# Dense feed-forwards that transpose x unnormalised and take up products of 512 columns

## Chip, cores and metric

The kernel runs on one core of one Trainium2 chip. Times are microseconds of device time for one execution. A time given for a kernel is the median of its runs; a profile is one further execution, whose own time stands beside its span.

## What is computed

256 tokens of 1024 features go through two blocks of two layers each. In the first block a layer is a mixer (a chunked recurrence, gates and a short convolution) and a feed-forward; the feed-forward of layer 0 is dense, that of layer 1 a mixture of 8 experts (MoE). Behind it stands a norm of its own. In the second block a layer is a dense feed-forward, a mixer of four branches and another dense feed-forward, each with a norm before and one after it. So there are five dense feed-forwards, and each is:

```
def rmsnorm(x, g):
    xf = x.astype(jnp.float32)
    y = xf * lax.rsqrt(jnp.mean(xf * xf, axis=-1, keepdims=True) + EPS)
    return (y * g.astype(jnp.float32)).astype(x.dtype)

def swiglu_ffn(h, w_gu, w_down):
    a, b = jnp.split(h @ w_gu, 2, axis=-1)
    return (jax.nn.silu(a) * b) @ w_down
```

with h = rmsnorm(x, g), 1024 features in, 2816 in the middle, 1024 out. All is float32.

## The kernel before

**Products.** Every float32 product is made of three: both operands are split into a high part that TensorE takes without loss and the remainder, and `mm3` (L205 to L209) issues high x high (L207), high x low (L208) and low x high (L209) into one PSUM tile. Weights arrive by SP's queue in raw tiles of 512 KB (`pump`, L111; seven buffers, issue in L124); ACT casts the high part (L139), DVE subtracts for the low part (L141), in pieces of 1024 columns, or two halves of 512 where a feed-forward or mixer begins; six such pairs exist. Activations are split by `split` (ACT L222, DVE L223).

**Layout.** 256 tokens are two tiles of 128 (token tile 0 and 1). A product contracts over 128 rows, so x has to stand with features on the partitions: `hT` is the pair (`hhi`, `hlo`) of eight blocks k of 128 features by 256 tokens.

**Entering a feed-forward.** `norm_next` and `prenorm` compute the mean square (ACT squares, L242; DVE L244), the factor (POOL, L226) and x times factor times gain (DVE L264), with a gain broadcast over the partitions that `gain` (L252 to L254) loads by POOL's queue. `put_hT` transposes four blocks at a time on TensorE (`turn`, L219) into one PSUM tile, which one cast and one subtraction of 512 columns bring into hT. For token tile 1 this is kept as `pend` and run once token tile 0's first products are issued.

**The feed-forward** (`ffn`, L419). The first 256 of 2816 features are computed token by token: hT is stationary, 256 weight columns move, a PSUM tile holds the tokens of one tile. The ten groups of 256 that follow are computed feature by feature: 128 x 128 weights are stationary, the 256 tokens of hT move; so g = silu(a) b comes out with features on the partitions, as the down products want it, and is split into arenas. Only the first group's g has to be transposed (`first_g`, L441). The down products have g as stationary and 512 weight columns moving; the last two chunks of them are done for token tile 0 first, so that its residual add (`add_post` L360, `norm_post` L370 and L373) and the next stage's entry run beside the products of tile 1.

**Out of the MoE.** `final_norm` (L1068) applies two norms in a row behind the add (L1008): squares (L1081), the gain (L1082), small sums on POOL (L1083 and on), squares again (L1091), the normalised x for the feed-forward (L1099), and the new x (L1105).

**Start.** `start` loads x and the first mixer's gain, 512 KB broadcast, then the weights; `enter_first` norms and transposes. `consts` loads small vectors by POOL's queue and turns them into columns.

The order of instructions on every engine is fixed before the run, by a planner that follows the order of the code, with side work (`spawn`, `step`) put later by a set amount of time.

## Time and profile before

| what | us |
|---|---|
| median of 3 runs | 2866.78 (2866.57 to 2866.88) |
| the profiled execution | 2866.45 |
| its span | 2864.7 |
| TensorE busy | 2800.7 (98%) |
| DVE busy | 2025.9 (71%) |
| ACT busy | 1644.8 (57%) |
| POOL busy | 85.7 (3%) |

From the span's start the stages lie at about: first mixer 0 to 322, dense feed-forward to 514, second mixer to 831, MoE to 1654, dense feed-forward to 1861, mixer to 2071, dense feed-forwards to 2263 and 2455, mixer to 2665, dense feed-forward to the end. Of TensorE's matmuls the profile gives starts that can be trusted and ends that are modelled, so the price of a product in a stream is the distance of two starts.

### The profile page before, as it was taken

How to read it: one execution, taken by the hardware profiler on the slowest of the kernel's cores; microseconds unless marked ns; L12 is line 12 of the kernel's file. 1: busy time of each engine (PE TensorE's matmuls, PEld its weight loads, DVE VectorE, ACT ScalarE, POOL GpSimd, SP SyncE). 2: the span in 40 equal slices, each digit the busy share in tenths (PEclk: the TensorE clock that was granted, in tenths of full speed). 3: DMA queues.
4: the chain of work that ended last, by engine and by line, in shares of the span. 5: the costliest groups of instructions: out<-in, count | busy, mean ns of one | idle time of the engine just before them, and what ended most of it. 6: DMA issues, size and time to landing. Idle time of an engine off the chain costs nothing. (4 is left out here: it accounts for less than half of the span.)

```text
span 2864.7 us, 47484 instructions
## 1 busy us (share of the span) xinstructions
PE 2800.7 (98%) x18688; PEld 2553.8 (89%) x18688; DVE 2025.9 (71%) x2639; ACT 1644.8 (57%) x2196; POOL 85.7 (3%) x162
## 2 busy tenths in 40 slices
PE   8999999999999999999999989999999999999999
PEld 8999998999988877877877789899999899899997
DVE  5766655675678888888888765578765555697654
ACT  6644544664458767777777654456544444565543
POOL 1000000000000000000000010100000001000000
PEclk9999999999999999999999989999999999999999
DMA  7554666555558999999999956664665566546553
GB/s 248 161 167 146 185 184 189 179 162 169 171 191 293 327 341 353 333 344 355 330 346 349 338 185 185 187 182 136 193 201 185 191 184 197 170 139 199 182 183 108
DMA packets 425047, 635.00 MB, mean 222 GB/s; under 512 B 20186, under 2 KB 298896, under 8 KB 424816
## 3 DMA queue, kind: packets, MB, share of 16 engines
q1 hardware_dynamic: 421184, 621.65, 67.0%
q0 software_dynamic: 3632, 10.24, 1.3%
q8 instruction: 148, 2.42, 0.4%
q14 instruction: 83, 0.68, 0.1%
HBM read 630.76 MB, written 1.05 MB: 221 GB/s over the span
## 5 line engine op out<-in xcount | busy, mean ns | idle before, releaser
L141 DVE TENSOR_TENSOR wl<-wr,wh 128x1024 fp32r<-128x1024 f32 (+2 forms) x1265 | 1408.3, 1139 | 602.6 <-ACT wh L139 592.5
L139 ACT CAST wh<-wr 128x1024 fp32r<-128x1024 f32 (+2 forms) x1265 | 1200.9, 983 | 626.7 <-PE mm L208 275.1
L207 PE MATMUL mm<-hhi,wh 128*128 128x256 f32 x3360 | 954.5, 284 | 0.0
L208 PE MATMUL mm<-hlo,wh 128*128 128x256 f32 x3360 | 953.2, 284 | 0.0
L209 PE MATMUL mm<-hhi,wl 128*128 128x256 f32 x3360 | 952.6, 284 | 0.0
L207 PEld LDWEIGHTS mm<-hhi,wh 128*128 128x128 f32 x3360 | 643.7, 192 | 1.2 <-issue 1.0
L208 PEld LDWEIGHTS mm<-hlo,wh 128*128 128x128 f32 x3360 | 643.8, 192 | 0.6 <-issue 0.3
L209 PEld LDWEIGHTS mm<-hhi,wl 128*128 128x128 f32 x3360 | 643.8, 192 | 0.6 <-issue 0.3
L208 PE MATMUL mm<-wl,a 128*128 128x512 f32 (+1 forms) x1336 | 514.0, 385 | 2.2
L207 PE MATMUL mm<-wh,a 128*128 128x512 f32 (+1 forms) x1336 | 509.7, 382 | 0.0
L209 PE MATMUL mm<-wh,a 128*128 128x512 f32 (+1 forms) x1336 | 508.5, 381 | 0.0
L208 PEld LDWEIGHTS mm<-wl,a 128*128 128x128 f32 x1336 | 251.3, 188 | 65.9 <-DVE wl L141 17.5
L207 PEld LDWEIGHTS mm<-wh,a 128*128 128x128 f32 x1336 | 251.4, 188 | 49.5 <-issue 1.6
L209 PEld LDWEIGHTS mm<-wh,a 128*128 128x128 f32 x1336 | 251.5, 188 | 45.6
L208 PE MATMUL sd<-wl,a 128*128 128x512 f32 x352 | 144.9, 412 | 1.1
L209 PE MATMUL sd<-wh,a 128*128 128x512 f32 x352 | 140.0, 398 | 5.1 <-PEq L1111 5.1
L207 PE MATMUL sd<-wh,a 128*128 128x512 f32 x352 | 117.4, 399 | 0.0
L222 ACT CAST a<-t 128x256 fp32r<-128x256 f32 (+1 forms) x114 | 49.3, 433 | 108.8 <-DVE t L460 105.4
L207 PE MATMUL mm<-a,wh 128*128 128x256 f32 x384 | 109.3, 285 | 0.0
L208 PE MATMUL mm<-a,wh 128*128 128x256 f32 x384 | 107.6, 280 | 0.0
L209 PE MATMUL mm<-a,wl 128*128 128x256 f32 x384 | 107.6, 280 | 0.0
L209 PE MATMUL mm<-wh,hlo 128*128 128x256 f32 x352 | 103.3, 294 | 3.5 <-DVE hlo L223 3.5
(319 smaller groups left out, 2486.1 us busy)
## 6 DMA issues: line engine op xcount, KB each, us to landing
wr<-in_expert_w_dram SPq DMA_DIRECT2D x515, 512.0 KB, 5.4
wr<-in_w_in_dram SPq DMA_DIRECT2D x240, 512.0 KB, 4.0
wr<-in_ffn_w_gu_dram SPq DMA_DIRECT2D x176, 512.0 KB, 3.7
wr<-in_ffn_w_down_dram SPq DMA_DIRECT2D x88, 512.0 KB, 3.7
wr<-in_dense_w_dram SPq DMA_DIRECT2D x66, 512.0 KB, 3.8
wr<-in_w_out_dram SPq DMA_DIRECT2D x32, 512.0 KB, 4.1
wr<-in_w_proj_conv_dram SPq DMA_DIRECT2D x16, 512.0 KB, 4.3
wr<-in_w_proj_hgrn_dram SPq DMA_DIRECT2D x16, 512.0 KB, 4.2
```

The lines of the kernel that those rows point to most:

```text
L139: nc.scalar.copy(hi[:, c:c + m], raw[:, c:c + m])
L141: nc.vector.tensor_sub(lo[:, c:c + m], raw[:, c:c + m], hi[:, c:c + m].bitcast(F32))
L207: mm(out, l[0], r[0], start=start, stop=False)
L208: mm(out, l[0], r[1], start=False, stop=False)
L209: mm(out, l[1], r[0], start=False, stop=stop)
L222: self.nc.scalar.copy(hi, src)
```

## The change

**Up products.** `UP_COLS` keeps the first 256 features and cuts the rest into five groups of 512. They are computed token by token: hT's 128 tokens are stationary, 512 weight columns move, one PSUM tile for each token tile, first for a, then for b. `stream` takes a piece of weights at a time. g comes out with tokens on the partitions; `turns` transposes it, four blocks into a PSUM tile, and splits it into the arenas, as side work.

**The norm.** `put_scaled` transposes x as it is and multiplies by the gain of a feature when the PSUM tile is read, one 128 x 128 block at a time (ACT `activation` with a scale of its own per partition, L389; DVE L390). The factor of a token is computed beside (`rf`), and enters as scale of the silu (L505) and in the multiplication (L507). `plain_next` does this in place of `norm_next` for the five dense feed-forwards, right behind the add.

**Out of the MoE** `final_norm` does `put_scaled` first, with the product of two gains, then both norms; its small sums move from POOL to DVE. **Start:** the gain comes as eight rows by ACT's queue and is transposed; x is normed without gain and goes through `put_scaled`. **Loads:** `gain` issues on SP's queue; five of its fifteen loads, and the start's, are gone, and `consts` has seven more small loads on POOL's queue instead.

```diff
-        self.nc.gpsimd.dma_start(t, ap.partition_broadcast(P))
+        self.nc.sync.dma_start(t, ap.partition_broadcast(P))
...
-    def enter_first(self, gt):
...
+    def enter_first(self, gain):
+        nc = self.nc
+        def normed(t):
+            r = self.mean_sq([self.x[:, t, h * 512:h * 512 + 512] for h in range(2)])
+            xs = self.t4()
+            for h in range(2):
+                sl = slice(h * 512, h * 512 + 512)
+                last = nc.vector.tensor_scalar_mul(xs[:, sl], self.x[:, t, sl], r)
+            return xs, last.ins
...
+        xs0, self.hold = normed(0)
+        self.pump(1)
+        self.hold = None
+        last = self.hold_act = self.put_scaled(0, gain, xs0)
+        self.pump(4)
+        self.hold_act = None
+        with self.tc.issue_after(last):
+            xs1, _ = normed(1)
+        self.pend = lambda: self.put_scaled(1, gain, xs1)
+        self.pump()
...
+    def put_scaled(self, t, gain, src=None):
+        hi, lo = self.hT
+        for h in range(2):
+            pt = self.sd_ps((P, 4, P))
+            self.turn(pt, (self.x[:, t, :] if src is None else src)[:, h * 512:(h + 1) * 512], 4)
+            for j in range(4):
+                k = 4 * h + j
+                sl = (slice(None), k, slice(t * P, t * P + P))
+                g = gain(k)
+                last = self.nc.scalar.activation(hi[sl], pt[:, j, :], AF.Copy, scale=g)
+                self.nc.vector.scalar_tensor_tensor(lo[sl], pt[:, j, :], g, hi[sl].bitcast(F32), ALU.mult,
+                                                    ALU.subtract)
+        return last.ins
...
+    def plain_next(self, gain):
+        def enter(t):
+            self.put_scaled(t, gain)
+            r = self.mean_sq([self.x[:, t, h * 512:(h + 1) * 512] for h in range(2)])
+            self.nc.vector.tensor_copy(self.rf[t], r)
+        def step(i):
+            if i == 1:
+                self.new_hT()
+                self.new_rf()
+                enter(0)
+            elif i == 2:
+                self.pend = lambda: enter(1)
+        return step
...
+    UP_COLS = [(0, 256)] + [(256 + j * 512, 512) for j in range(5)]
...
-            self.add((n, "a", g), wa[:, :, sl])
-            self.add((n, "b", g), wb[:, :, sl])
+        for g, (c0, cn) in enumerate(self.UP_COLS):
+            self.add((n, "a", g), wa[:, :, c0:c0 + cn])
+            self.add((n, "b", g), wb[:, :, c0:c0 + cn])
         for g in range(KF // 2):
...
+        def swiglu(out, t, a, b):
+            if b is None:
+                nc.scalar.activation(out, a, AF.Silu, scale=rf[t])
+            else:
+                nc.vector.scalar_tensor_tensor(out, b, rf[t], out, ALU.mult, ALU.mult)
...
+        def turns(t, k0, nb, sa):
+            pt = self.sd_ps((P, 4, P))
+            self.turn(pt, sa, nb)
+            yield
+            b = 0
+            while b < nb:
+                i, r = (k0 + b) // 8, (k0 + b) % 8
+                m = min(nb - b, 8 - r)
+                sl = (slice(None), slice(r, r + m), slice(t * P, t * P + P))
+                self.split(G[0][i][sl], G[1][i][sl], pt[:, b:b + m, :])
+                b += m
+            yield
...
-                for p in self.take((n, c, g)):
-                    self.fm_piece([(b, pt[:, j, :]) for b, pt in enumerate(pts)], p, self.hT_all, KD)
...
+        for g, (c0, cn) in list(enumerate(self.UP_COLS))[1:]:
+            sas = [self.t2((P, 512)) for _ in range(NT)]
+            for c in "ab":
+                pts = [self.mm_ps() for _ in range(NT)]
+                for k0, kn, hi, lo in self.stream((n, c, g)):
+                    for t in range(NT):
+                        for kk in range(kn):
+                            k = k0 + kk
+                            self.mm3(pts[t], self.hT_tok(k, t), (hi[:, kk, :], lo[:, kk, :]), k == 0, k == KD - 1)
+                    self.done()
+                for t in range(NT):
+                    if c == "a":
+                        swiglu(sas[t], t, pts[t], None)
+                    else:
+                        swiglu(sas[t], t, None, pts[t])
+                        spawn(t, c0, cn, sas[t])
+                yield
...
-        nc.sync.dma_start(gt, first_gain.partition_broadcast(P))
-        self.pump(2)
+        nc.scalar.dma_start(rows[0:KD, :], first_gain.rearrange("(b p) -> b p", p=P))
+        self.dmas(2)
...
+        gains = (I["norm_ffn"][1], I["norm_ffn"][0], I["ffn1_pre_g_2"][0], I["ffn1_pre_g_2"][1],
+                 I["ffn2_pre_g_2"][0], I["ffn2_pre_g_2"][1])
+        for i, v in enumerate(gains):
+            put(rows1[74 + 8 * i:82 + 8 * i, :], v.rearrange("(b p) -> b p", p=P))
...
+            if nxt is not None:
+                self.put_scaled(t, self.fin_g)
...
-            nc.gpsimd.tensor_scalar(ss[:, 0:1], ss[:, 0:1], ss[:, 1:2], EPS, ALU.add, ALU.add)
+            nc.vector.tensor_scalar(ss[:, 0:1], ss[:, 0:1], ss[:, 1:2], EPS, ALU.add, ALU.add)
...
-            for h in range(2):
-                nc.scalar.activation(junk[:, sl[h]], w[:, sl[h]], AF.Square, scale=1.0 / 32.0, accum_out=sw[:, h:h + 1])
-            nc.gpsimd.tensor_scalar(sw[:, 0:1], sw[:, 0:1], sw[:, 1:2], r, ALU.add, ALU.mult)
-            nc.gpsimd.tensor_scalar(sw[:, 0:1], sw[:, 0:1], r, EPS, ALU.mult, ALU.add)
-            r2 = self.col()
-            self.rsqrt(r2, sw[:, 0:1])
-            nc.gpsimd.tensor_tensor(r2, r2, r, ALU.mult)
-            xs = self.t4()
-            for h in range(2):
...
+                nc.vector.tensor_scalar(sw[:, 0:1], sw[:, 0:1], sw[:, 1:2], r, ALU.add, ALU.mult)
+                nc.vector.tensor_scalar(sw[:, 0:1], sw[:, 0:1], r, EPS, ALU.mult, ALU.add)
+                r2 = self.col()
+                self.rsqrt(r2, sw[:, 0:1])
+                nc.vector.tensor_mul(self.rf[t], r2, r)
```

In a feed-forward's up products TensorE had before, for one group, feature by feature (`mm` the PSUM tile, `wh` and `wl` the weights' parts; the third feed-forward):

```order
L207 MATMUL mm_25088<-hhi_24862,wh_24916 128x256
L208 MATMUL mm_25088<-hlo_24863,wh_24916 128x256
L209 MATMUL mm_25088<-hhi_24862,wl_24917 128x256
L207 MATMUL mm_25088<-hhi_24862,wh_24916 128x256
L208 MATMUL mm_25088<-hlo_24863,wh_24916 128x256
L209 MATMUL mm_25088<-hhi_24862,wl_24917 128x256
L207 MATMUL mm_25088<-hhi_24862,wh_24916 128x256
L208 MATMUL mm_25088<-hlo_24863,wh_24916 128x256
L209 MATMUL mm_25088<-hhi_24862,wl_24917 128x256
```

and has now, in the same feed-forward, token by token (`t` is g of the group before):

```order
L226 MATMUL mm_24495<-wh_24377,hhi_23985 128x512
L227 MATMUL mm_24495<-wl_24378,hhi_23985 128x512
L228 MATMUL mm_24495<-wh_24377,hlo_23986 128x512
L238 MATMUL sd_24403<-ident,t_4557_24249 128x128 x4
L226 MATMUL mm_24496<-wh_24377,hhi_23985 128x512
L238 MATMUL sd_24410<-ident,t_4558_24250 128x128 x4
L227 MATMUL mm_24496<-wl_24378,hhi_23985 128x512
L228 MATMUL mm_24496<-wh_24377,hlo_23986 128x512
L226 MATMUL mm_24496<-wh_24377,hhi_23985 128x512
L227 MATMUL mm_24496<-wl_24378,hhi_23985 128x512
```

Three products of 512 columns take the place of six of 256, and bursts of four transposes stand between them.

At the entry of the same feed-forward (`a` the mixer's arena, `x` the residual stream) TensorE had before:

```order
L209 MATMUL mm_24714<-wh_24746,a_4439_24388 128x512
L207 MATMUL mm_24715<-wh_24746,a_4438_24387 128x512
L208 MATMUL mm_24715<-wl_24747,a_4438_24387 128x512
L209 MATMUL mm_24715<-wh_24746,a_4439_24388 128x512
L219 MATMUL sd_24864<-ident,t_4511_24835 128x128 x4
L219 MATMUL sd_24871<-ident,t_4511_24835 128x128 x4
L207 MATMUL mm_24942<-wh_24764,hhi_24862 128x256
L208 MATMUL mm_24942<-wl_24765,hhi_24862 128x256
L209 MATMUL mm_24942<-wh_24764,hlo_24863 128x256
```

and has now, still among the mixer's last products of token tile 1:

```order
L227 MATMUL mm_23847<-wl_23836,a_4434_23520 128x512
L228 MATMUL mm_23847<-wh_23835,a_4435_23521 128x512
L226 MATMUL mm_23848<-wh_23835,a_4434_23520 128x512
L227 MATMUL mm_23848<-wl_23836,a_4434_23520 128x512
L238 MATMUL sd_23987<-ident,x 128x128 x4
L228 MATMUL mm_23848<-wh_23835,a_4435_23521 128x512
L238 MATMUL sd_24000<-ident,x 128x128 x4
L226 MATMUL mm_23847<-wh_23861,a_4434_23520 128x512
L227 MATMUL mm_23847<-wl_23862,a_4434_23520 128x512
L228 MATMUL mm_23847<-wh_23861,a_4435_23521 128x512
```

The transposes moved from behind the last mixer product to 13 products ahead of it, and read x itself.

DVE had there before:

```order
L373 SCALAR_TENSOR_TENSOR x<-t_4504_24816,col_24822,x 128x512 x2
L141 TENSOR_TENSOR wl_24901<-wr_24665,wh_24900 128x512 x2
L244 TENSOR_SCALAR col_24828<-col_24828 128x1
L141 TENSOR_TENSOR wl_24909<-wr_24685,wh_24908 128x512
L264 SCALAR_TENSOR_TENSOR t_4511_24835<-x,col_24833,gain_22452 128x512 x2
L370 TENSOR_TENSOR t_4516_24878<-mm_24714,gain_22450 128x512
L244 TENSOR_SCALAR col_24879<-col_24879 128x1
L223 TENSOR_TENSOR hlo_24863<-sd_24864,hhi_24862 128x4x128
L370 TENSOR_TENSOR t_4516_24878<-mm_24715,gain_22450 128x512
L223 TENSOR_TENSOR hlo_24863<-sd_24871,hhi_24862 128x4x128
```

and has now:

```order
L448 SCALAR_TENSOR_TENSOR x<-t_4500_23949,col_23955,x 128x512 x2
L150 TENSOR_TENSOR wl_24034<-wr_23798,wh_24033 128x512 x2
L390 SCALAR_TENSOR_TENSOR hlo_23986<-sd_23987,cols,hhi_23985 128x128
L390 SCALAR_TENSOR_TENSOR hlo_23986<-sd_24000,cols,hhi_23985 128x128
L263 TENSOR_SCALAR col_24013<-col_24013 128x1
L150 TENSOR_TENSOR wl_24042<-wr_23818,wh_24041 128x512
L390 SCALAR_TENSOR_TENSOR hlo_23986<-sd_23987,cols,hhi_23985 128x128
L390 SCALAR_TENSOR_TENSOR hlo_23986<-sd_24000,cols,hhi_23985 128x128
L405 COPY rfs<-col_24018 128x1
L150 TENSOR_TENSOR wl_24050<-wr_23839,wh_24049 128x512
L390 SCALAR_TENSOR_TENSOR hlo_23986<-sd_23987,cols,hhi_23985 128x128
L390 SCALAR_TENSOR_TENSOR hlo_23986<-sd_24000,cols,hhi_23985 128x128
```

The subtractions of 512 columns (L223) became eight of 128 (L390), in pairs from two PSUM tiles, with weight splits (L150, before L141) between the pairs; the multiplication by gain and factor (L264) is gone.

Out of the MoE, ACT had before (`x` behind the MoE's add):

```order
L139 CAST wh_20260<-wr_16304 128x512 x2
L139 CAST wh_20274<-wr_16316 128x512 x2
L1081 ACTIVATE t_3861_20340,col_20338<-x 128x512 x2
L139 CAST wh_20288<-wr_16335 128x512
L1091 ACTIVATE t_3861_20340,col_20339<-t_3858_20337 128x512 x2
L139 CAST wh_20288<-wr_16335 128x512
L1105 ACTIVATE x<-t_3858_20337,col_20346 128x1024
L139 CAST wh_20302<-wr_16353 128x512 x2
L139 CAST wh_20316<-wr_16379 128x512
L222 CAST hhi_20358<-sd_20360 128x4x128
L139 CAST wh_20316<-wr_16379 128x512
L222 CAST hhi_20358<-sd_20367 128x4x128
```

and has now:

```order
L148 CAST wh_19846<-wr_15890 128x512 x2
L148 CAST wh_19860<-wr_15902 128x512 x2
L1193 ACTIVATE t_3863_19954,col_19952<-x 128x512
L389 ACTIVATE hhi_19923<-sd_19925,fing 128x128
L148 CAST wh_19874<-wr_15921 128x512
L389 ACTIVATE hhi_19923<-sd_19938,fing 128x128
L148 CAST wh_19874<-wr_15921 128x512
L389 ACTIVATE hhi_19923<-sd_19925,fing 128x128
L389 ACTIVATE hhi_19923<-sd_19938,fing 128x128
L1193 ACTIVATE t_3863_19954,col_19952<-x 128x512
L389 ACTIVATE hhi_19923<-sd_19925,fing 128x128
L389 ACTIVATE hhi_19923<-sd_19938,fing 128x128
```

The evictions of x(0) (L389) moved ahead of the second norm's squares (before L1091, now L1201) and of the new x.

## Rows read from the trace of the kernel before

**Rows 1.** The page's part 1: busy time, share and instructions of TensorE.

```profile
PE 2800.7 (98%) x18688; PEld 2553.8 (89%) x18688; DVE 2025.9 (71%) x2639; ACT 1644.8 (57%) x2196; POOL 85.7 (3%) x162
```

**Rows 2.** Windows, TensorE alone: up products, first dense feed-forward (window, length, busy, clock, DMA).

```profile
322.50:437.60 115.10, 114.39 (x941) 1.00 0.64 187
```

**Rows 3.** One line's instructions, L207, three windows: count, ns min/median/max, first and last start.

```profile
L207 PE MATMUL mm<-hhi,wh x168: 283/283/283, 359.8 to 419.9; 128*128 128x256 f32 x168
...
L207 PE MATMUL mm<-wh,a x21: 389/389/389, 476.0 to 489.6; 128*128 128x512 f32 x21
...
L207 PE MATMUL mm<-wh,a x26: 389/389/389, 495.0 to 512.3; 128*128 128x512 f32 x26
```

**Rows 4.** Timeline of TensorE, first dense feed-forward (start, length, instruction).

```profile
345.59 0.28 PE L209 MATMUL mm<-hhi,wl 128*128 128x256 f32 x1
345.71 0.60 PE L441 MATMUL sd<-ident,t 128*128 128x128 f32 x4
...
346.38 0.29 PE L209 MATMUL mm<-hhi,wl 128*128 128x256 f32 x1
```

**Rows 5.** Timelines of ACT, DVE and TensorE, start (last: idle before, releaser).

```profile
10.21 1.14 ACT L139 CAST wh<-wr 128x512 fp32r<-128x512 f32 x2 [5.36 <-DMA wr<-in_w_in_dram]
...
11.46 1.41 DVE L264 SCALAR_TENSOR_TENSOR t<-x,col,gain 128x512 f32<-128x512 f32 x2
...
12.27 1.97 PE L219 MATMUL sd<-ident,t 128*128 128x128 f32 x8 [12.27 <-DVE t L264]
...
16.25 0.58 PE L209 MATMUL mm<-wh,hlo 128*128 128x256 f32 x1 [0.73 <-DVE hlo L223]
...
19.61 0.41 PE L209 MATMUL mm<-wh,hlo 128*128 128x256 f32 x1
```

**Rows 6.** Out of the MoE: windows, TensorE's waits (us, times, longest), timelines of DVE, TensorE.

```profile
1655.60:1662.10 6.50, 0.02 (x1) 0.71 0.51 160
1662.10:1668.60 6.50, 5.94 (x25) 0.50 0.44 145
...
PE sd L219 <- DVE t L1099: 8.7, 2, 6.5
...
1654.74 1.44 DVE L1008 SCALAR_TENSOR_TENSOR x<-mm,Sc,x 128x512 f32<-128x512 f32 x2 [0.22 <-PE mm L203]
...
1683.57 0.28 PE L209 MATMUL mm<-wh,hlo 128*128 128x256 f32 x1
```

**Rows 7.** Entries behind a mixer: windows, timelines of TensorE and DVE.

```profile
2068.00:2078.00 10.00, 8.82 (x58) 1.00 0.33 104
2261.00:2271.00 10.00, 8.81 (x61) 1.00 0.32 107
2663.00:2673.00 10.00, 8.82 (x60) 1.00 0.31 107
...
2070.23 0.39 PE L209 MATMUL mm<-wh,a 128*128 128x512 f32 x1
2071.55 1.32 PE L219 MATMUL sd<-ident,t 128*128 128x128 f32 x8 [0.94 <-DVE t L264]
...
2073.61 0.38 PE L209 MATMUL mm<-wh,hlo 128*128 128x256 f32 x1 [0.22 <-DVE hlo L223]
...
2066.89 1.42 DVE L373 SCALAR_TENSOR_TENSOR x<-t,col,x 128x512 f32<-128x512 f32 x2
2068.22 1.29 DVE L141 TENSOR_TENSOR wl<-wr,wh 128x512 fp32r<-128x512 f32 x2
```

**Rows 8.** Lines L966, L967 (as rows 3), and a group by form (busy us, mean ns).

```profile
L966 ACT ACTIVATE a<-mm,cols x32: 466/476/493, 840.7 to 1399.9; 128x256 fp32r<-128x256 f32 x32
...
  DVE a L967: 2.4, 3
...
L967 DVE SCALAR_TENSOR_TENSOR a<-mm,cols,a x32: 473/479/484, 841.2 to 1401.6; 128x256 fp32r<-128x256 f32 x32
...
L1600 ACT ACTIVATE t<-t,col 128x128 f32<-128x128 f32 x8 | 3.1, 392 | 0.0
```

More of the change, by code (lines that the diff above doesn't have):

```diff
@@ L107, in add, with dmas, pump @@
         self.plan.append((key, first, len(self.pieces)))
-    def pump(self, limit=1 << 30):
+    def dmas(self, n):
+        for i in range(n):
+            ap, kn, cols = self.raws[i]
+            raw = self.ring.tile([P, RAW], F32, name=self.nm("wr"), tag="wr", bufs=RAW_BUFS)
+            self.nc.sync.dma_start(raw[:, :kn * cols].rearrange("p (k c) -> p k c", c=cols), ap)
+            self.raw[i] = raw
+        self.dma_i = n
+    def pump(self, upto=1 << 30):
         nc = self.nc
+        after = lambda ins: self.tc.issue_after(ins) if ins is not None else nullcontext()
         while True:
             moved = False
-            if self.dma_i >= limit:
-                return
             i = self.dma_i
@@ L138, in pump @@
                     for c in range(0, n, m):
-                        nc.scalar.copy(hi[:, c:c + m], raw[:, c:c + m])
-                        with self.tc.issue_after(self.hold) if self.hold is not None else nullcontext():
+                        with after(self.hold_act):
+                            nc.scalar.copy(hi[:, c:c + m], raw[:, c:c + m])
+                        with after(self.hold):
                             nc.vector.tensor_sub(lo[:, c:c + m], raw[:, c:c + m], hi[:, c:c + m].bitcast(F32))
@@ L170, in take, with stream @@
         return [self.parts.pop(i) for i in range(a, b)]
+    def stream(self, key):
+        k, a, b = self.plan[self.next_i]
+        assert k == key, (k, key)
+        self.next_i += 1
+        for i in range(a, b):
+            self.pump()
+            assert i < self.split_i, (key, i, self.split_i, self.freed)
+            yield self.parts.pop(i)
     def done(self, n=1):
@@ L466, in lhs @@
         def lhs(k, t):
+            for key in [key for key in late if key[0] <= k + 4]:
+                self.finish(late.pop(key))
             hi, lo = g_at(k)
@@ L1656, in build @@
                 self.plan_ffn((kind, l), gu[:, 0:DFF], gu[:, DFF:2 * DFF], I[n + "_w_down_2"][l])
[L1657 to L1661 removed]
+        gain = self.start(I[stages[0][2]][stages[0][1]])
+        self.enter_first(gain)
         late = self.spawn(self.consts())
```

102 lines of the change are left out of this document (47 added, 55 removed).

## Prediction, made before the changed kernel had run

> **What bounds the kernel now.** I read the page's head first: TensorE is busy for 2800.7 of 2864.7 us [rows 1]. So time can only come from two places: from how long the products themselves take, and from the few stretches in which TensorE waits. The five dense feed-forwards are read next. In the first one the up products fill 115.1 us with TensorE busy for 114.39 of them [rows 2]: there is no wait in there to win, only the price of a product. That price is the distance of starts: 168 L207 products with 256 columns start from 359.8 to 419.9, and each is one of three, so 60.1/167/3 = 0.120 us [rows 3]. In the down products of the same feed-forward, 512 columns each, 21 starts lie between 476.0 and 489.6, so 13.6/20/3 = 0.2267 us, and later, on the third pair of arenas, 26 between 495.0 and 512.3, 17.3/25/3 = 0.231 us [rows 3]. Twice 256 columns cost 0.240 us, once 512 cost 0.227 to 0.231. Third, I read the stretches in which TensorE stands: the start, the way out of the MoE, and the entries of the feed-forwards behind a mixer.
>
> **The up products.** Per feed-forward 320 x 3 = 960 products of 256 columns become 480 of 512; the first 256 features stay as they were. Before: 960 x 0.120 = 115.2 us, which is what [rows 2] shows. After, at 0.2267 us: 108.8 us; at 0.231: 110.9 us. Saved: 6.4 or 4.3 us. Which one applies is not shown, as no product of before has 512 columns with the normalised x (hhi, hlo) as its stationary tile. 0.120 and 0.2267 are both the columns at 2.4 GHz (0.107, 0.213) plus 0.013 us, so I take 0.2267.
>
> Against it stand the transposes: g now comes out token by token and is turned back, 44 transposes a feed-forward instead of 4. Four of them in the stream take L209's start at 345.59 to the next L209's at 346.38; three products would have taken 0.36, so four cost 0.79 - 0.36 = 0.43 us, 0.108 each [rows 4]. 40 x 0.108 = 4.3 us. They wait for nothing: in the changed order they stand about 50 products behind the group whose g they turn, some 11 us, in which ACT and DVE have one silu and one multiplication per tile. Net: 6.4 - 4.3 = 2.1 us per feed-forward, 10 us in five; at 0.231 the net is nothing, and at 0.236 (as much again above) five lose 12 us.
>
> The two evictions of a transposed block cost ACT and DVE time, not TensorE's: 1024 columns of weights are split in about the time of two 512-column halves, 1.29 us on DVE [rows 7], and a block of four transposes adds one cast and one subtraction of 512 columns to each engine every 5 us; meanwhile TensorE needs 12 x 0.2267 = 2.7 us for 1024 columns of weights. Neither engine becomes the bound.
>
> The Trainium skill, "TensorE: Matmul & The Clock Gate", section "Back-to-back issue gap", has columns/2.4 GHz + 2.5 ns. By it 960 products would take 104.8 us and 480 would take 103.6: the wider form would save 1.2 us, the transposes would eat it, and five feed-forwards would lose 16 us. By [rows 3] the extra is 0.013 us, so the trace speaks against the rule; it is the fourth rival.
>
> **The start.** TensorE's first real run of products begins at 16.25, behind the norm with a 512 KB gain (L264 at 11.46), the transposes (12.27) and the evictions; it runs at half clock, 16 steps from 16.25 to 19.61, 0.21 us each [rows 5]. The first four blocks (12 products) are done near 18.5. After, no gain is loaded that way; ACT casts the first weights (10.21, 1.14 us [rows 5]) and then does eight evictions. ACT and DVE alternate on a bank: the nearest rows are 0.477 and 0.479 us for 256 columns and 0.392 us for 128 columns on ACT [rows 8], and I take 0.45 for one 128-column eviction with its hand-over. Two banks overlap, so a block of the order k0, k4, k1, k5 comes out every 0.9 us of pairs: k0 is ready at 10.21 + 1.14 + 0.9 = 12.25, k3 at 14.95, its three products end at 15.6. That is 2.9 us sooner than 18.5. The 512 KB that stood ahead of the weights in SP's queue are gone, so the cast itself comes sooner; I add 0.6: 3.5 us. Bounds: nothing, if the small loads of the constants (more of them, on the same POOL queue) stall the products a little later; and 6.0, if the products start at 10.21.
>
> **Out of the MoE.** TensorE does nothing from 1655.6 to 1662.1, then works at half clock to 1668.6, and waits once more behind it; both waits are for L1099, the second norm, 8.7 us in two waits. The last product of the feed-forward's first group starts at 1683.57 [rows 6]. In the new order x(0) is transposed straight after the MoE's add, and both norms run beside the products. x(0) is ready near 1656.2 (L1008, 1654.74 + 1.44). On DVE eight evictions (8 x 0.45) stand with four halves of weight splits (4 x 0.65 [rows 7]) between: 6.2 us behind the first split at 1657.4, so k7 is ready near 1663.5 and tile 0's 48 products end between 1667 (full clock) and 1671 (half). x(1)'s add stands on DVE behind the norm work of tile 0, and its evictions end near 1677; TensorE fills the gap with products of the next group for tile 0, which need nothing of x(1). I put the end of the first group at 1679.8, with 21 products of the next group done (21 x 0.2267 = 4.8 us) where before has three of the old form (0.4). Gain: 3.9 + 4.8 - 0.4 = 8.3 us. Bounds: 4 (the half clock lasts as long as now and x(1) comes as late as now) and 11.
>
> **The entries behind a mixer.** At 2070.23 the last down product starts, at 2071.55 the transposes, at 2073.61 the first lo product [rows 7]. Without waits this last start would be 0.23 + 8 x 0.108 + 0.24 = 1.3 us behind 2070.23; it is 3.4 behind, 2.0 us lost at x(0). The other two entries look the same (8.82, 8.81 and 8.82 us busy in 10 [rows 7]). After, the transposes of x(0) need only the add (L373, 2066.89 to 2068.31) and stand 13 products ahead of the mixer's end, so that wait goes. What is late next: DVE reaches the first eviction at 2069.5, behind a split; with the splits in its order between each two pairs, k2 and k3 come out near 2072.9 and 2074.2, 1.8 us of waits for TensorE. At x(1) I expect what is lost now, less 0.2, as its add is as early as before and its evictions are longer. A gain of 0.4 us each, 1.2 for three; between -2 and +1.5 each. The entry of the first feed-forward, behind the same kind of mixer: nothing, within 1 us. The gains' own loads move from POOL's queue to SP's, where they stand in line with the weights and wait for DVE to free a gain tile; seven raw buffers stand ahead, each the work of 2.7 us, so a wait under some 19 us reaches nobody, and I price it at nothing.
>
> **Sum.** 10.2 + 3.5 + 8.3 + 1.2 = 23.2 us from the profiled execution's 2866.45 gives 2843.3; the median of the runs is 0.3 above it: 2843.5 us.
>
> **Rivals.**
> - The wide products run at 0.231, like the late down products: transposes and products cancel, 10.2 us are missing: 2854. For it: the row exists, in the same feed-forward; against it: only one of three arenas shows it. 0.17.
> - The start and the MoE's way out give nothing, because x(1), the loads or the half clock end last there as they do now: 2843.5 + 11.8 = 2855. For it: half the stretch after 1662.1 is at half clock today whatever is ready. Against it: the waits named are for L264 and L1099, which leave the path. 0.12; together with the first: 2865.5, 0.03.
> - Slower: the small evictions pace every entry. Each of six places (start, MoE, four entries) has two tiles of eight pairs, where two casts and two subtractions stood. At 0.45 us an eviction I have them neutral; if the hand-over between ACT and DVE and the weight splits queued among them make it 0.80, each place loses 8 x 2 x 0.35 = 5.6 us, 33.6 in six: 2877. It decides from 0.45 + 29/96 = 0.75 us on. For it: eight hand-overs a tile stand where there were two; against it: L966 and L967 do just this with 256 columns in 0.48 us, and of 32 casts three waited for L967, 2.4 us together [rows 8]. 0.06.
> - The wide product saves only 0.0025 us on two narrow ones: 0.2375, so 480 take 114.0 us, with the transposes 3.1 more than now, 15.6 in five, instead of 10.2 less: 2869. Against it: no row of 512 columns is above 0.231 [rows 3]. 0.03. It is what the rule of the section "Back-to-back issue gap" of the Trainium skill, "TensorE: Matmul & The Clock Gate", would make of it.
> - A transpose costs more between 512-column products than between 256-column ones: at 0.275 us, 40 x 0.167 = 6.7 us in each feed-forward, 33 us: 2877. Against it: [rows 4]. 0.02. The Trainium skill, "TensorE: Matmul & The Clock Gate", section "Part 4: PE-mode transpose", gives about 275 ns in one kernel's context; this trace has 0.108.
> - The change does more than I see (loads gone from the queue, more products to fill waits): under 2835. 0.05.
>
> **How the numbers follow.** My forecast, 2843.5, between 2835 and 2851 by itself, has 0.52. The range for 8 in 10 reaches down to 2833 and up to 2858, over the first two rivals. A measurement of this kernel can tell 0.2%, 5.7 us, from no change. Faster by more than that (under 2861): 0.52 + 0.17 + 0.12 + 0.05, less 0.02 for the upper ends of the rivals, 0.84. Same: 0.09 (0.03 + 0.03 + 0.02 and a little). Slower: 0.07.
>
> **What would show it.** In the changed profile: the L226 products with 512 columns and hhi as stationary tile 0.227 us apart (0.231: the first rival); a burst of four L238 transposes adding 0.43 us; the up products with their transposes near 113 us per feed-forward instead of 115; TensorE's first products near 12 us and a first wait behind the MoE of about 2 us in place of 6.5; the end of that first group near 1680 less what came before; waits for L389 and L390 of about 2.9 us at an entry. I am wrong if waits for L390 grow past 5 us an entry, or if TensorE's queue waits for SP's weights behind a gain.

## The result, and the profile after

The changed kernel takes 2837.99 us (median of 4 runs, 2836.27 to 2841.31), the kernel before beside it on the same chip 2866.68 (2863.5 to 2866.88): a ratio of 0.9904, with a 95% interval from 0.9887 to 0.9921. That is 28.7 us gained, 5.5 more than the forecast. The time lies inside the range, and what was forecast as likeliest happened. The profiled execution took 2837.38 us with a span of 2835.6, 29.1 less than that of before.

The page's part 1, first line, as [rows 1]: TensorE has 2199 instructions fewer, is still busy for 98%, and gave up 11.2 us of busy time; the other 17.9 us of the shorter span are time in which it stood before.

```profile
PE 2789.5 (98%) x16489; PEld 2445.3 (86%) x16489; DVE 2019.0 (71%) x2635; ACT 1659.0 (59%) x2193; POOL 76.9 (3%) x146
```

**Up products.** Instructions of L226 on TensorE in the first dense feed-forward (as [rows 3]: count, ns, first and last start, shapes), then its timeline there (as [rows 4]: start, length, instruction), in two stretches, without and with a burst of transposes:

```profile
L226 PE MATMUL mm<-wh,hhi x192: 277/389/477, 324.6 to 449.3; 128*128 128x512 f32 x160, 128*128 128x256 f32 x32
```

```profile
355.66 0.39 PE L228 MATMUL mm<-wh,hlo 128*128 128x512 f32 x1
...
361.78 0.39 PE L228 MATMUL mm<-wh,hlo 128*128 128x512 f32 x1
...
371.30 0.39 PE L228 MATMUL mm<-wh,hlo 128*128 128x512 f32 x1
371.53 0.60 PE L238 MATMUL sd<-ident,t 128*128 128x128 f32 x4
371.88 0.47 PE L226 MATMUL mm<-wh,hhi 128*128 128x512 f32 x1
372.20 0.60 PE L238 MATMUL sd<-ident,t 128*128 128x128 f32 x4
372.55 0.47 PE L227 MATMUL mm<-wl,hhi 128*128 128x512 f32 x1
372.86 0.39 PE L228 MATMUL mm<-wh,hlo 128*128 128x512 f32 x1
```

From 355.66 to 361.78 there are 27 steps: 6.12/27 = 0.2267 us a product. From 371.30 to 372.86 stand three products and eight transposes: 1.56 - 3 x 0.227 = 0.88 us for two bursts, 0.44 each (0.43 was forecast). From the first up product (324.6) to the first down product (450.0) it takes 125.4 us; in the kernel before it is 128.4, from 327.15 to 455.58. Of these 3.0 us 0.9 comes back behind, since the last group's eight transposes now stand among the down products. This distance is the one to compare: the window of [rows 2] is not the up products alone, as it begins with the mixer's last 12 products and ends 18 us ahead of the first down product.

**Out of the MoE.** TensorE's waits from 1645 to 1682 (total, times, longest), and windows of TensorE there (window, length, busy and instructions, granted clock, DMA share, GB/s), to be set beside [rows 6]:

```profile
PE mm L226 <- ACT hhi L389: 0.8, 2, 0.6
PE mm L228 <- DVE hlo L390: 0.5, 1, 0.5
PE mm L222 <- ACT a L241: 0.2, 1, 0.2
```

```profile
1650.00:1653.00 3.00, 2.29 (x14) 1.00 0.01 3
1653.00:1656.00 3.00, 2.10 (x8) 1.00 0.73 202
1656.00:1660.00 4.00, 4.00 (x35) 1.00 0.64 208
```

The wait of 6.5 us is gone, and with it the half clock behind it: the granted clock stays at 1.00 (2.4 GHz) where 0.50 stood. What is left are 1.3 us for the small evictions L389 and L390.

**Entry behind a mixer.** TensorE's one wait from 2050 to 2065, where [rows 7] lost 2.0 us at token tile 0 alone; then DVE at the same place (start, length, instruction) and the evictions of this kind as a whole (count, busy, mean ns, idle before):

```profile
PE mm L226 <- ACT hhi L389: 0.3, 1, 0.3
```

```profile
2052.32 0.61 DVE L390 SCALAR_TENSOR_TENSOR hlo<-sd,cols,hhi 128x128 fp32r<-128x128 f32 x2
...
2053.67 0.60 DVE L390 SCALAR_TENSOR_TENSOR hlo<-sd,cols,hhi 128x128 fp32r<-128x128 f32 x2
...
2055.13 0.61 DVE L390 SCALAR_TENSOR_TENSOR hlo<-sd,cols,hhi 128x128 fp32r<-128x128 f32 x2
...
2056.26 0.60 DVE L390 SCALAR_TENSOR_TENSOR hlo<-sd,cols,hhi 128x128 fp32r<-128x128 f32 x2
```

```profile
L389 ACT ACTIVATE hhi<-sd,cols 128x128 fp32r<-128x128 f32 x64 | 20.9, 372 | 2.8 <-DVE hlo L390 2.8
L390 DVE SCALAR_TENSOR_TENSOR hlo<-sd,cols,hhi 128x128 fp32r<-128x128 f32 x64 | 19.8, 345 | 1.4 <-ACT hhi L389 1.2
```

**Start.** TensorE's waits up to 40 us, and two of its instructions:

```profile
PE sd L238 <- DVE t L316: 3.9, 2, 3.5
PE sd L582 <- DMA t<-in_norm_mix_dram: 3.2, 1, 3.2
PE sd L613 <- DMA t<-in_conv_dw_dram: 0.9, 1, 0.9
PE sd L612 <- issue: 0.9, 1, 0.9
PE mm L228 <- DVE hlo L390: 0.2, 1, 0.2
```

```profile
9.01 0.58 PE L226 MATMUL mm<-wh,hhi 128*128 128x256 f32 x1
...
15.32 0.34 PE L226 MATMUL mm<-wh,hhi 128*128 128x256 f32 x1
```

And two pairs of evictions on DVE there, 0.78 us apart, with no split between:

```profile
9.59 0.60 DVE L390 SCALAR_TENSOR_TENSOR hlo<-sd,gcol,hhi 128x128 fp32r<-128x128 f32 x2
10.37 0.61 DVE L390 SCALAR_TENSOR_TENSOR hlo<-sd,gcol,hhi 128x128 fp32r<-128x128 f32 x2 [0.18 <-ACT hhi L389]
```

The products begin at 9.01 and run at full clock from 15.32 on, where before their long run began at 16.25 and was still at half clock at 19.61 [rows 5]. But TensorE then waits at the transposes of the constants (L612, L613), 1.8 us in all, for their loads.

**Where the time went, by stage.** For every kernel I took the starts of the first 512-column product of each out projection and down projection as marks, and compare the distances between them. The up term is in all five dense feed-forwards; the stages differ in what else the change does there. (`plain_next` serves four of the five, those behind a mixer or a feed-forward; the one behind the MoE is entered by `final_norm`.)

| stage, us | before | after | new up loop alone (e1) | old entries (e4) | old MoE exit (e5) | old start (e6) |
|---|---|---|---|---|---|---|
| start to first out projection | 303.6 | 301.8 | 303.6 | 301.6 | 302.1 | 303.2 |
| first dense feed-forward, entry and up | 151.9 | 148.2 | 149.4 | 149.3 | 148.2 | 148.2 |
| its down, second mixer | 350.6 | 351.7 | 350.0 | 351.8 | 351.8 | 350.3 |
| MoE, up to its last expert's down | 737.2 | 737.4 | 737.2 | 738.1 | 737.8 | 737.4 |
| MoE's end, exit and up | 255.5 | 241.8 | 252.2 | 244.2 | 248.6 | 241.6 |
| down, mixer, layer 0 | 249.8 | 250.7 | 250.7 | 250.6 | 250.6 | 250.6 |
| entry and up | 154.1 | 149.5 | 150.9 | 150.8 | 149.2 | 149.3 |
| down, entry and up | 192.4 | 188.5 | 190.1 | 190.0 | 188.5 | 188.5 |
| down, mixer, layer 1 | 248.0 | 248.9 | 248.9 | 248.8 | 248.9 | 248.9 |
| entry and up | 154.1 | 149.2 | 150.9 | 150.8 | 149.2 | 149.2 |

### The profile page after: what moved, and what is told of

Read it like the earlier page. It is cut to its first block, busy times and chain, and to the rows that moved or that the text cites. A ratio compares the mean times of both kernels' runs of the same rounds, so it can differ in the third digit from the quotient of the medians.

```text
span 2835.6 us, 43057 instructions
## 1 busy us (share of the span) xinstructions
PE 2789.5 (98%) x16489; PEld 2445.3 (86%) x16489; DVE 2019.0 (71%) x2635; ACT 1659.0 (59%) x2193; POOL 76.9 (3%) x146
## 5 line engine op out<-in xcount | busy, mean ns | idle before, releaser
L150 DVE TENSOR_TENSOR wl<-wr,wh 128x1024 fp32r<-128x1024 f32 (+2 forms) x1265 | 1409.4, 1140 | 617.4 <-ACT wh L148 609.6
L226 PE MATMUL mm<-wh,a 128*128 128x512 f32 (+1 forms) x1336 | 509.8, 382 | 0.0
L226 PE MATMUL mm<-hhi,wh 128*128 128x256 f32 (+1 forms) x1760 | 501.8, 285 | 0.0
L227 PE MATMUL mm<-hlo,wh 128*128 128x256 f32 (+1 forms) x1760 | 500.5, 284 | 0.0
L228 PE MATMUL mm<-hhi,wl 128*128 128x256 f32 (+1 forms) x1760 | 499.9, 284 | 0.0
L226 PE MATMUL mm<-wh,hhi 128*128 128x512 f32 (+1 forms) x1152 | 415.0, 362 | 2.0 <-ACT hhi L389 1.6
L228 PE MATMUL mm<-wh,hlo 128*128 128x512 f32 (+1 forms) x1152 | 412.6, 360 | 1.3 <-DVE hlo L390 0.7
L227 PE MATMUL mm<-wl,hhi 128*128 128x512 f32 (+1 forms) x1152 | 413.7, 360 | 0.1
L226 PEld LDWEIGHTS mm<-hhi,wh 128*128 128x128 f32 (+1 forms) x1760 | 336.6, 191 | 1.2 <-issue 1.0
L227 PEld LDWEIGHTS mm<-hlo,wh 128*128 128x128 f32 (+1 forms) x1760 | 336.5, 191 | 0.6 <-issue 0.3
L228 PEld LDWEIGHTS mm<-hhi,wl 128*128 128x128 f32 (+1 forms) x1760 | 336.6, 191 | 0.6 <-issue 0.3
L226 PEld LDWEIGHTS mm<-wh,a 128*128 128x128 f32 x1336 | 251.3, 188 | 49.3 <-issue 1.7
L226 PEld LDWEIGHTS mm<-wh,hhi 128*128 128x128 f32 x1152 | 218.1, 190 | 36.5 <-ACT hhi L389 4.9
L227 PEld LDWEIGHTS mm<-wl,hhi 128*128 128x128 f32 x1152 | 218.2, 190 | 31.0 <-DVE wl L150 0.4
```

The lines of the kernel that those rows point to most:

```text
L150: nc.vector.tensor_sub(lo[:, c:c + m], raw[:, c:c + m], hi[:, c:c + m].bitcast(F32))
L226: mm(out, l[0], r[0], start=start, stop=False)
L227: mm(out, l[0], r[1], start=False, stop=False)
L228: mm(out, l[1], r[0], start=False, stop=stop)
```

## Experiments

Theory: the gain is the sum of separate terms, wide products less transposes (10), MoE exit (8), start (3), entries (a little). Rivals: the small evictions have no slack and would turn any place into a loss; the width gives nothing; the gain comes from somewhere else (loads, queues). Of each kernel the text of its expectation stands as it was before the run. The kernel before ran beside each of them; its medians lie between 2865.8 and 2866.9 us, so differences between kernels of different groups are good to about 1 us.

### e1: the new up loop alone

In the kernel before, `plan_ffn` and `ffn` of the kernel after; x is normalised ahead of the transposes as before, so the factor is 1.

```diff
-        for g in range(KF // 2):
+        for g, (c0, cn) in enumerate(self.UP_COLS):
...
+        rf = [1.0] * NT
```

> The kernel before with the new up products alone (first 256 features, then five groups of 512 token by token, g transposed); norms, entries, start and loads as before. The forecast's first term says 10.2 us less than before, 2856.5 us: products at 0.227 us give 6.4 us a feed-forward, 40 transposes take 4.3 back. The rival (products at 0.231, as late in the down products) says no change, 2866.7. A third reading, that the up loop only pays together with the new entries, would show less than 5 us.

2853.86 us (5 runs, 2852.99 to 2856.37), ratio to before 0.996 [0.9946, 0.9975]: 12.1 us. In the table, a stage with up products alone is 2.3 to 3.3 us shorter, and 0.9 comes back in the stage behind it, since the last group's eight transposes stand among the down products. Not all of the 12.1 belongs to the up loop. In the profiles, where e1's span is 12.7 shorter than that of before, TensorE waits 3.8 us instead of 5.1 at a branch of the MoE, and the second mixer is 0.6 shorter although the 0.9 has moved into it, as the clock does not fall there (both in the last section): 1.3 and 1.5 us, which leave about 10. By this run the term is there at the size forecast.

### e2 and e3: the two halves of that term

e2 keeps everything of the kernel after but the width: eleven groups of 256 columns, still token by token.

```diff
-    UP_COLS = [(0, 256)] + [(256 + j * 512, 512) for j in range(5)]
+    UP_COLS = [(j * 256, 256) for j in range(11)]
...
```

> The changed kernel with up products of 256 columns instead of 512, still token by token and with all the transposes (11 groups of 256). By the forecast what is won is the width alone: 480 x (2 x 0.120 - 0.227) = 6.2 us a feed-forward, 31 in five, 2869 us. If the gain came from the layout (weights moving instead of stationary) and not from the width, the time stays near 2838.

e3 leaves out the transposes of the five wide groups, so that the down products get g as it stands, with the tokens on the partitions (other numbers, the same work).

```diff
-            pt = self.sd_ps((P, 4, P))
-            self.turn(pt, sa, nb)
+            if nb == 4:
+                pt = sa.rearrange("p (b n) -> p b n", n=P)
+            else:
+                pt = self.sd_ps((P, 4, P))
+                self.turn(pt, sa, nb)
```

> The changed kernel with the 40 transposes per feed-forward of the wide groups left out: g is split from where it lies, without being turned, so the down products get other numbers. By the forecast 40 x 0.108 = 4.3 us a feed-forward, 21.6 in five, 2816 us. If a transpose hid in the stream it would be less (2830 and up); at 0.275 us each it would be 55 us, 2783.

e2 takes 2868.35 us (10 runs, 2865.52 to 2871.08), 1.0007 [0.9997, 1.0016] of before: without the width the whole change is worth nothing. Its products stand 0.120 us apart, as these rows of its timeline in the first feed-forward show; so it is the form, 512 columns against twice 256, and not the layout or the operand held still that makes them cheaper. e3 takes 2813.85 us (4 runs), 0.9817 [0.98, 0.9833].

```profile
358.11 0.28 PE L227 MATMUL mm<-wl,hhi 128*128 128x256 f32 x1
358.23 0.28 PE L228 MATMUL mm<-wh,hlo 128*128 128x256 f32 x1
```

So the width is worth 30.4 us (2868.35 - 2837.99; forecast 5 x 6.4 = 32) and the 200 transposes cost 24.1, 0.12 us each (forecast 0.108, 21.6). The difference, 6.2, is less than what e1 gave. By the marks, with the second mixer's clock left out, it is about 7, against the 10 of e1. What makes the remaining 3 us is open; each figure in the runs is a difference of medians whose runs lie up to 5 us apart. So the net of this term is known only as 6 to 10 us.

### e4, e5, e6: one place put back to the old form in each

e4 gives the four entries behind a mixer or a feed-forward their old code, e5 the old `final_norm`, e6 the old `start` and `enter_first`; all else is as after.

```diff
e4
-                elif (nk, nl) in self.PLAIN:
+                elif kind != "mix1" and kind != "mix2" and kind != "ffb" and (nk, nl) in self.PLAIN:
e5
-            if nxt is not None:
-                self.put_scaled(t, self.fin_g)
...
+            xs = self.t4()
+            for h in range(2):
+                nc.vector.scalar_tensor_tensor(xs[:, sl[h]], w[:, sl[h]], r2, gt[:, sl[h]], ALU.mult, ALU.mult)
...
+                self.put_hT(0, xs)
...
e6
...
-        last = self.hold_act = self.put_scaled(0, gain, xs0)
+        xs0 = self.prenorm(0, gt)
+        self.put_hT(0, xs0)
...
```

> The changed kernel with the four entries behind a mixer or a feed-forward as before (norm factor and gain applied ahead of the transposes, gains loaded by SP's queue, two wide evictions). By the forecast these entries are worth 1.2 us in all: 2839 us. The changed kernel's trace shows TensorE losing 0.6 to 0.8 us at three of them where it lost 3.2 before, and 0.7 less at the first: by that 8 us, 2846 us.

> The changed kernel with the way out of the MoE as before (both norms ahead of the transposes, small sums on POOL). By the forecast 8.3 us slower than the changed kernel, 2846.3 us. From the stage marks of the two traces (13.7 us won between the MoE's last expert and the next down products, of which about 2 belong to the up products and 1.6 to a branch of the MoE that nothing of the change touches) about 10, 2848 us.

> The changed kernel with the start as before (512 KB gain by SP ahead of the weights, norm with gain, two wide evictions). The forecast has 3.5 us for the start, 2841.5 us. The traces have the first out-projection of the mixer begin 1.8 us sooner, as TensorE waits for the small loads of the constants (2 us near 28); with the old start that wait may shrink, so by the trace 1 to 2 us, 2839 to 2840.

| kernel | us (4 runs) | ratio to before | dearer than after | in its own stages |
|---|---|---|---|---|
| e4 old entries | 2845.51 (2844.21 to 2846.65) | 0.9929 [0.9913, 0.9946] | 7.5 | 1.1 + 1.3 + 1.5 + 1.6 = 5.5 |
| e5 old exit | 2846.41 (2844.55 to 2849.57) | 0.9937 [0.992, 0.9953] | 8.4 | 6.8 |
| e6 old start | 2837.00 (2836.89 to 2840.67) | 0.9905 [0.9888, 0.9921] | -1.0 | 1.4 |

TensorE's waits in e4 at the entry behind the mixer of layer 0, then in e5 behind the MoE, with one of e5's windows there, then in e6 at the start, with the second transpose of the constants in the kernel after and in e6:

```profile
PE sd L238 <- DVE t L283: 0.9, 1, 0.9
PE mm L228 <- DVE hlo L242: 0.2, 1, 0.2
```

```profile
PE sd L238 <- DVE t L1209: 7.0, 2, 6.5
```

```profile
1656.50:1664.00 7.50, 6.96 (x31) 0.50 0.47 138
```

```profile
PE sd L238 <- DVE t L283: 12.0, 1, 12.0
PE sd L591 <- DMA t<-in_conv_dw_dram: 0.6, 1, 0.6
```

```profile
30.68 0.30 PE L613 MATMUL sd<-ident,t 128*128 128x128 f32 x1 [0.91 <-DMA t<-in_conv_dw_dram]
```

```profile
30.74 0.30 PE L591 MATMUL sd<-ident,t 128*128 128x128 f32 x1 [0.56 <-DMA t<-in_conv_dw_dram]
```

e5 brings back the 6.5 us wait and the half clock behind it, as [rows 6]. e4 brings back the wait for the normalised x; of its 7.5 us 5.5 lie in the four entries, and 1.7 belong to a branch that has nothing to do with the edit (last section). e6 waits 12.0 us for its first transposes, and its start stage is only 1.4 us longer. In both kernels TensorE is held until the same load of constants lands: the second transpose runs at 30.68 in the kernel after and at 30.74 in e6. What remains of the early start is that 115 products are done by then instead of 104, and 11 x 0.12 = 1.3 us. That e6 is nevertheless as fast as a whole has nothing to do with the start: in its profile the second mixer is 1.4 us shorter, as the clock does not fall there (last section). The parts add up to 27.0 of the 28.7 us (12.1 + 7.5 + 8.4 - 1.0), but as they hold some 3 us of the branch and the clock in e1, 1.7 of the branch in e4 and 1.4 of the clock in e6, their sum proves little. Behind the MoE they do not add up: the kernel after is 13.7 us faster there than before, the branch makes 1.6 of it, the up loop 2.0 (e1's 3.3 less its 1.3 of branch), and the 10 that are left are 3 more than e5 brings back. e5 is not quite the old exit: its two waits for x are 7.0 us together, those of before 8.7 [rows 6].

### e7: have the small evictions any slack?

Every L389 and every L390 is issued twice.

```diff
-                last = self.nc.scalar.activation(hi[sl], pt[:, j, :], AF.Copy, scale=g)
+                for _ in range(2):
+                    last = self.nc.scalar.activation(hi[sl], pt[:, j, :], AF.Copy, scale=g)
+                for _ in range(2):
+                    self.nc.vector.scalar_tensor_tensor(lo[sl], pt[:, j, :], g, hi[sl].bitcast(F32), ALU.mult,
...
```

> The changed kernel with each small eviction (the cast with gain on ACT and the subtraction on DVE, 16 pairs at each of six places) done twice, so an eviction takes about 0.3 us longer on each engine. If the evictions pace the entries, as in the slower rival, each place loses about 8 x 2 x 0.3 = 4.8 us, 29 us in six, 2867. If TensorE has cover for most of them it loses 1 to 2 us a place, 2844 to 2850.

2867.47 us (10 runs, 2865.43 to 2869.37), 1.0004 [0.9995, 1.0014] of before: 29.5 us dearer than after, the whole gain. By the marks 7.0 at the start, 1.9 at the first feed-forward, 4.9 behind the MoE, 5.9, 5.9 and 5.5 at the other three entries, less 1.4 in the second mixer, where the clock does not fall in e7. TensorE's waits at the entry behind the mixer of layer 0 (2050 to 2085; in e7 the evictions are L390 on ACT and L392 on DVE) and three windows of TensorE there:

```profile
PE mm L228 <- DVE hlo L392: 1.5, 2, 0.7
PE mm L226 <- ACT hhi L390: 1.1, 1, 1.1
PE sd L238 <- DVE hlo L392: 0.2, 1, 0.2
```

```profile
2066.00:2070.00 4.00, 2.36 (x12) 1.00 0.43 131
2070.00:2074.00 4.00, 2.84 (x10) 0.67 0.39 126
2074.00:2078.00 4.00, 4.00 (x20) 0.50 0.47 138
```

Two things make up most of the 5.9 us: the waits, 2.8 (0.3 in the kernel after), and what follows them, a fall of the granted clock to 0.50 (1.2 GHz) for some 7 us, in which a product of 256 columns takes 0.21 us instead of 0.12 [rows 3, 5]: 7 x (1 - 0.12/0.21) = 3.0. So there is little cover at five of the six places; the first feed-forward's entry has more. How much slower the evictions could be before the clock falls no run shows.

### e11: the gains' queue

The loads of `gain` go back to POOL's queue, all else as after.

```diff
-        self.nc.sync.dma_start(t, ap.partition_broadcast(P))
+        self.nc.gpsimd.dma_start(t, ap.partition_broadcast(P))
```

> The changed kernel with the gains' loads issued by POOL's queue as before. The forecast prices the move to SP's queue at nothing: 2838 within 1 us. If a gain ahead of the weights in SP's queue holds weights back, this is faster by 1 us or more.

2837.34 us (4 runs, 2835.51 to 2838.16), 0.9898 [0.9881, 0.9914]. Nothing, as priced.

### e8, e9, e10, e12: is more to be had?

e8 puts the even and the odd blocks of x into the two PSUM tiles of a transposed x, everywhere, so that consecutive blocks come out of two tiles; e9 loads the gains in a third set of rows behind the other constants; e10 does both; e12 does e8's at the three entries behind mixer and feed-forward and at the first feed-forward alone.

```diff
e8, e10 (e12 the same behind a switch)
-            self.turn(pt, (self.x[:, t, :] if src is None else src)[:, h * 512:(h + 1) * 512], 4)
...
+                pt[:, j, :], xs[:, (2 * j + h) * P:(2 * j + h + 1) * P], self.ident), 4)
...
-                k = 4 * h + j
+                k = 2 * j + h
e9, e10
...
-        for i, v in enumerate(gains):
-            put(rows1[74 + 8 * i:82 + 8 * i, :], v.rearrange("(b p) -> b p", p=P))
...
+        rows3 = self.t2((P, P))
...
+        for i, v in enumerate(gains):
+            put(rows3[8 * i:8 * i + 8, :], v.rearrange("(b p) -> b p", p=P))
```

> The changed kernel with the even blocks of x in one PSUM tile and the odd ones in the other, so that the evictions, which alternate between the tiles, come out as k0, k1, k2, k3 and not as k0, k4, k1, k5; the products take them in that order. The changed kernel's trace has TensorE wait 0.6 to 0.8 us for L389 and L390 at the entries and about 1.3 at the MoE's way out: if it waits for the order, 2 to 4 us less, 2834 to 2836. If it waits for the first blocks or for x's second half (which the even tile now needs too), no change or 1 us more.

> The changed kernel with the constants loaded in two parts: the seven loads that the kernel before had, and the gains of the feed-forwards in a tile of their own behind them. The changed kernel's trace has TensorE wait 2.1 us near 28 us for the constants' transposes, which the kernel before does not show. If the added loads cause it, 2 us less, 2836; if POOL's order of issue does, no change.

> Both edits together, even and odd tiles and constants in two parts. If both hold, 4 to 6 us less than the changed kernel, 2832 to 2834; if neither, 2838.

> The changed kernel with even and odd blocks of x in one PSUM tile each, at the entries behind a mixer or a feed-forward alone; start and way out of the MoE stay as in the changed kernel, and the order of TensorE's instructions is the same but there. In the profiles of the two kernels with the edit everywhere, the stages from those entries to the next down products were 1.2, 0.8 and 0.9 us shorter than in the changed kernel (and the first unchanged), while the start and the way out were 1 to 5 us longer. If the waits at the entries come from the order of the evictions, these three stages are shorter again by 2.9 us in all, 2835 us; if they move with the planner's order instead, no change.

| kernel | us | ratio to before |
|---|---|---|
| e8 | 2841.60 (5 runs, 2838.43 to 2843.15) | 0.9913 [0.9899, 0.9926] |
| e9 | 2840.22 (4 runs, 2839.0 to 2840.66) | 0.9909 [0.9894, 0.9924] |
| e10 | 2838.33 (4 runs, 2838.06 to 2840.03) | 0.9905 [0.989, 0.992] |
| e12 | 2836.98 (4 runs, 2836.05 to 2838.85) | 0.9897 [0.9879, 0.9914] |

None is better than the kernel after by more than the runs scatter. TensorE's waits, one of each view: e8 at the start, e8 behind the MoE, e9 at the start:

```profile
PE sd L614 <- issue: 4.8, 1, 4.8
```

```profile
PE sd L385 <- DVE x L1120: 2.3, 1, 2.3
```

```profile
PE sd L607 <- DMA t<-in_ffn_pre_g_dram: 2.8, 1, 2.8
```

Behind the MoE, even blocks need both halves of x, so the transposes wait 2.3 us for the second half of the add, which the order by halves doesn't. At the three entries behind mixer and feed-forward e12 gains 0.9, 0.8 and 0.9 us by the marks (2.9 in all was expected if the order is what TensorE waits for), and e8 and e10 gain 0.7 to 1.1 at the same three. So the order of the blocks does cost something there, but too little to be told from noise in the runs; in e12's profile the start (1.0) and the MoE's end (2.9, of which 1.8 is the branch of the last section) take it back. At the start the wait for the constants only moves: with the gains loaded apart, the transposes of the other constants (L607) come 5 us sooner, at 24.56, and wait 2.8 us there. The page puts this wait down to a gain's load, but the gains' own transpose (L662, at 42.93) waits for nothing. In e6 the wait is short (0.6 us) because TensorE gets there later, as said above. In the kernel before it is nothing: POOL issues the last of its seven loads at 20.67, against 24.62 with seven more, and the transposes come at 31.05.

## Why the prediction was right

- **Up products (forecast 10.2; e1 12.1 in the runs and about 10 in the profile, by e2 and e3 6.2).** The choice of 0.2267 over 0.231 was right: 27 new products in a row keep 0.2267, the width gives 30.4 of the 32 us forecast (e2), and the first rival falls. The burst cost 0.44 instead of 0.43. One reading was wrong and did no harm: the 115.2 us of the 960 products follow from the price, but [rows 2] does not show them, as its window holds only some 810 of them, beside the first 256 features and the end of the mixer. The Trainium skill, "TensorE: Matmul & The Clock Gate", section "Back-to-back issue gap", gives columns/2.4 GHz + 2.5 ns for the gap of an isolated product; taken for this stream, it would have made the wide form save almost nothing (an estimate: 0.2158 us against twice 0.1092). Measured are 0.2267 and 0.120. The same page's "Part 4: PE-mode transpose" has about 275 ns for a bf16 transpose in one kernel's context; in this stream a float32 one costs 0.11 to 0.12 us (e3), so the fifth rival falls too.
- **MoE exit (8.3; e5 6.8 by the marks and 8.4 in the runs, about 10 against before).** The mechanism is the one forecast. x(0) is ready at 1650.9 (1656.2 before, 1650.4 in e5). The first product comes at 1651.39 (1663.91 before, 1658.10 in e5), and the last one of the first group at 1672.76, with 21 products of the next group ahead of it, as many as forecast, against 1675.91 and 2 in e5. What the forecast did not have is that the clock never falls: it allowed for an end of tile 0 at half clock.
- **Start (3.5; e6 1.4 by the marks).** This step failed towards its lower bound, which had been named: the small loads of constants stall the products. The first products were forecast near 12.25 and come at 9.01, but TensorE then stands at L612 and L613, 1.8 us, until the last load lands, which in e6 holds it 0.6 us. The sum took the gain at the front and only bounded the loss behind it; what came through is the 11 products done by then.
- **Entries (1.2; 5.5).** The mis-sized step. (The product at 2070.23, called a down product there, belongs to the mixer's out projection, and the second of the three entries lies behind a feed-forward.) It gave the vanished wait at x(0) back almost wholly, as 1.8 us of waits for k2 and k3, and left x(1) nearly as it was. In the trace, TensorE's time over its products from the last out-projection products to the end of x(1)'s evictions is 4.5 us in e4 and 3.1 in the kernel after, with the 16 transposes in both (16 x 0.108 = 1.7): 2.8 us of loss became 1.4. The blocks come out every 1.13 to 1.46 us with splits between (2052.32, 2053.67, 2055.13, 2056.26), close to what was assumed, but a pair of evictions takes 0.61 us and not 2 x 0.45, and TensorE asks for the first block later, as the transposes now stand among the products ahead of it. The first feed-forward's entry, priced at nothing, gave 1.1.
- **Gains' queue (0; e11: -0.65, within the scatter).** Right.
- **The slower rival** put a pace of 0.75 us as the point of decision. The pace was put at 0.45 us an eviction with its hand-over and is 0.39 where no split stands between (a pair every 0.78 us, 9.59 and 10.37). e7 shows that its mechanism is real: doubled evictions cost 29.5 us, where a pace of 0.75 was priced at 29. That the two agree so well is partly luck: the places lose 1.9 to 7.0 us instead of 4.8 each, and at the entry shown above about half of the loss is not the pace but the clock that falls behind the waits.

The total came out closer than its parts, and that is luck: by the marks 2.1 us too much at the start stand against 4.3 too little at the entries, the exit lies between 1.5 below its forecast and 2 above it, and the up products between 0 and 4 below. And 1.6 us of the profile's 29 are not the change's at all: the branch named below waits that much less in it than in that of before.

## What to carry to other kernels

Where TensorE is busy throughout, read the price of a product from its start-to-start distance by form; here each product took 0.013 us more than its columns at 2.4 GHz (0.120 and 0.2267 us against 0.107 and 0.213), which made twice 256 columns dearer than once 512, and that paid for 40 transposes a feed-forward. A wait ahead of TensorE can cost as much again when the clock falls behind it (2.8 us of waits and 3.0 of half clock in e7), so take out the long ones first, and test by doubling a suspected cost whether its cover is real before calling it hidden. When a gain is moved to the front of a program, ask which load the products will now reach too early.

## What the runs showed of the hardware that I had not expected

- **A branch that waits differently from kernel to kernel.** At the end of the experts TensorE's sequencer waits at a branch. The same row (TensorE's waits, 1600 to 1645 or 1650) of the kernels before, after and e4:

```profile
PE sd L209 <- PEq L1111: 5.1, 1, 5.1
```

```profile
PE sd L228 <- PEq L1225: 3.5, 1, 3.5
```

```profile
PE sd L228 <- PEq L1225: 5.2, 1, 5.2
```

  e8 (5.1) and e12 (5.3) are with the long ones, all others lie between 3.3 (e6, e7) and 4.1 (e9); no edit lies there. What decides it stays open.
- **A clock that falls or doesn't behind nearly the same wait.** In the second mixer TensorE waits for the same line in every kernel, 3.5 us in two waits in before and e1, 3.9 in after. Windows of TensorE there in before, after and e1:

```profile
772.00:775.00 3.00, 3.00 (x19) 0.61 0.56 175
```

```profile
766.00:769.00 3.00, 2.44 (x12) 0.56 0.11 22
```

```profile
769.00:772.00 3.00, 2.83 (x24) 1.00 0.27 42
```

  Where the clock stays at 1.00 (e1, e6, e7) the stage is 350.0 to 350.3 us long, where it falls (after, e4, e5) 351.7 or 351.8; before falls too, at 350.6, without the 0.9 us that the new up loop moves into this stage. With the branch this makes some 3 us of difference between profiles that no edit explains, as much as the smaller terms of the sum. Whether it belongs to the kernel or to the one execution that was profiled is not shown; runs of one kernel lie up to 5 us apart.
- **Two small evictions in a row overlap on one engine.** A pair of L390 on DVE takes 0.60 to 0.61 us, not 2 x 0.345, so its second starts about 0.26 us behind its first.
